# A hybrid attention layer on one Trainium2 core: matrix units moved between attention steps, x transposed two blocks at a time, one softmax sum folded into the norm

## Chip, cores and metric

The kernel runs on one core of one Trainium2 chip. The metric is the device time of one execution in microseconds (us), the median of several runs. All matrix products run on TensorE (PE in the profile); VectorE is DVE, ScalarE is ACT, GpSimd is POOL, and SP issues most of the loads.

## What is computed

One layer of a decoder for T = 512 positions and a width D of 1024, in float32. Cut to what matters:

```python
xn   = rmsnorm(h, g_attn)
proj = xn @ w_in                # q, k, v of 8 stick-breaking heads; q, k of 8 maps and v of 4 differential heads
sb   = stick_breaking(q, k, v)  # A[t,s] = beta_ts * prod over s<j<t of (1 - beta_tj), beta = sigmoid(z)
diff = (softmax(Q1 K1' / 8 + b1) - lam * softmax(Q2 K2' / 8 + b2)) V     # per head: two maps, 64 columns each
diff = rmsnorm(diff, g_subln) * (1 - lambda_init)
h    = h + concat(sb, diff) @ w_o
u    = causal_depthwise_conv3(rmsnorm(h, g_ffn) @ w_up)
h    = h + (gelu(gate) * val) @ w_down
h    = h + sigmoid(rmsnorm(h, g_ple) @ w_ple_gate) * (p @ w_ple_proj)
out  = rmsnorm(h, g_final)
```

`b1` and `b2` are biases by distance from a table of 32 rows; `lam` comes from four vectors of 64 numbers. All EPS are 1e-6.

## The kernel before

**Products.** A float32 product is made of three products of parts: each operand is split into a high part (`whi`, `xgh`, ...), a cast on ScalarE, and a low part (`wlo`, `xgl`, ...), a subtraction on VectorE. `mm3` (lines 119 to 123) issues the three matmuls. The attention's q, k and x come with 128 partitions by 512 positions in a tile.

**Weights as units.** `add_qk`, `add_v` and `add_wo` queue the projections as pieces. Their flow is a generator, and one `next` of it is a unit: one `mm3`, three matmuls of 512 columns. `units(n)` takes n of them from the flow; `rest()` takes what is left. Before a piece is used, its weights are loaded on SP's queue (`wraw`, line 131) and split (lines 140 and 141), two pieces ahead.

**Order.** TensorE's order is written by hand: it is the order of the code. The order on VectorE, ScalarE, GpSimd and SP is set by the scheduler of the framework, by priorities and by what a step needs. PSUM has two pools of tiles, `mm` (one bank, four tiles) and `z` (two banks, two tiles); which banks each gets is set by the one that is asked for first.

**Start** (`stages`, lines 715 to 772). x comes in four transfers. `warm(24)` runs 24 matmuls on an identity, `params_attn` transposes the gain `gattn`, and then `prep_x` (line 312) transposes a block of 128 columns of x into a PSUM bank and reads it twice, for `xgh` on ScalarE and `xgl` on VectorE. Two blocks share a tile `z`. `keep_x` reads it a third time and keeps a copy `xc` in DRAM for the residual. The first q and k products run between the later blocks. Then `units(8)`.

**Stick-breaking pairs** (`pair_steps`, line 535). A pair of heads goes through five steps: logits of two groups of rows with their sigmoids, scans and betas (`sb_sticks`, lines 510 to 518); the third group; transposes of the betas (line 562) in two steps; and `av` (line 574), whose eviction is two ScalarE copies (line 580) and two VectorE additions (line 581). A table `plan` of (pair, step, units) sets how many units follow each step.

**Parameters** (`params`, line 199) brings gains, convolution weights, the lambda vectors and the bias table; it transposes rows (lines 217 and 218), makes `sk` by two small matmuls (line 252) and copies it into `sk2` in DRAM (line 257), from which each head loads two strips on SP (line 595). It runs behind step 0 of pair 0.

**Differential heads** (`diff_steps`, line 587). Per row block and map: logits plus strip with a running minimum (line 618), exp with a row sum `sm` (line 622). The second map is scaled on ScalarE (line 627), and a VectorE operation scales the first and adds (line 628). Then transposes, `av`, the squares' sum by a matmul with ones (line 657), `rsqrt` (line 146), and the scaling by a broadcast row. A `plan` of (head, units) follows.

**Residual** (`residual`, line 668). An output tile is added to `hT` (line 671) on VectorE, then split into `h1` (lines 674 and 675). Behind the last of the eight tiles a new PSUM pool `psB` begins (line 826), and the up projection starts with its first two tiles.

Of the kernel before, what the change touches and what calls it, by code (L numbers as in the profile page):

```python
# [11 lines left out]
F32 = mybir.dt.float32  # L12
F32R = mybir.dt.float32r
AF = mybir.ActivationFunctionType
ALU = mybir.AluOpType
# [3 lines left out]
P = 128  # L19
T = 512  # L20
# [21 lines left out]
class Kern:  # L42
# [269 lines left out]
    def prep_x(self, pst):  # L312

        nc = self.nc
        self.xg_pool = self.open("xg", side="left")
        self.rst_pool = self.open("rst", side="left")
        self.xt_d = self.dram.tile([KT, P, T], F32, name="xt_d")
        self.xg = []
        for k in range(KT):
            ps = pst()  # L320
            for tb in range(NB):
                nc.tensor.transpose(ps[:, tb * P : (tb + 1) * P], self.xn[:, tb, k * P : (k + 1) * P], self.ident)
            hi = self.xg_pool.tile([P, T], F32R, name=f"xgh{k}")
            lo = self.xg_pool.tile([P, T], F32R, name=f"xgl{k}")
            g = self.gattn[:, k : k + 1]
            nc.scalar.activation(hi, ps, AF.Copy, scale=g)
            nc.vector.scalar_tensor_tensor(lo, ps, g, hi.bitcast(F32), op0=ALU.mult, op1=ALU.subtract)  # L327
            self.xg.append((hi, lo))
            yield ps

    def keep_x(self, k, ps):
        nc = self.nc
# [254 lines left out]
    def diff_steps(self, hd):  # L587
# [21 lines left out]
        for tb in (3, 2, 0, 1):  # L609
            if tb == 1:  # L610
                yield
                z.append(self.logits(q, k, groups[2]))
            n = (tb + 1) * P
            ts = [tiles[tb, j] for j in range(2)]
            bank, col = where[tb]
            for j in range(2):
                t = ts[j]
                nc.vector.tensor_tensor_reduce(
                    out=t, in0=z[bank][:, j, col : col + n], in1=strips[j][:, T - n : T], scale=-1.0, scalar=3e38,
                    op0=ALU.add, op1=ALU.min, accum_out=nm[:, j, tb : tb + 1],  # L620
                )
                nc.scalar.activation(t, t, AF.Exp, scale=-1.0, bias=nm[:, j, tb : tb + 1], accum_out=sm[:, j, tb : tb + 1])
            r = self.small.tile([P, 2], F32, tag="rsm", name=self.nm("rsm"))
            nc.vector.reciprocal(r, sm[:, :, tb])
            r1 = self.small.tile([P, 1], F32, tag="rlm", name=self.nm("rlm"))
            nc.vector.tensor_mul(r1, r[:, 1:2], self.neglam)
            nc.scalar.activation(ts[1], ts[1], AF.Copy, scale=r1)
            nc.vector.scalar_tensor_tensor(ts[0], ts[0], r[:, 0:1], ts[1], op0=ALU.mult, op1=ALU.add)
            pr[tb] = ts[0]
        yield  # L630

# [23 lines left out]
        ps = zo[:, 1, :] if hd == NDH - 1 else self.psm()  # L655
        for tb in range(NB):
            nc.tensor.matmul(ps[:, tb : tb + 1], lhsT=sq[:, tb * P : (tb + 1) * P], rhs=self.ones[:, 0:1], start=True, stop=True)
        rc = self.small.tile([P, NB], F32, tag="rcd", name=self.nm("rcd"))
        self.rsqrt(rc, ps[:, 0:NB], 1.0 / P)
        yield  # L660
        self.bcast_row(rc, ps)
        nc.vector.tensor_mul(o, ps, o)
# [32 lines left out]
    def stages(self):  # L695
# [18 lines left out]
        self.qks, self.v, self.hT, self.qk, self.late = {}, [None, None], None, None, []  # L714
        self.xn = self.su.tile([P, NB, D], F32, name="xn")
        self.load_x((0,))
        busy = self.psm()

        def warm(n):
            for _ in range(n):  # L720
                nc.tensor.matmul(busy[:, :P], lhsT=self.identR, rhs=self.identR, start=True, stop=True)

        warm(24)
        self.params_attn(psh)

        def first_load():
            cols = self.qk_cols(self.qoff[0], self.koff[0])
# [15 lines left out]
        self.add_wo(0, False, self.half_out)  # L743
        self.add_wo(4, True, lambda nt, ps: self.residual(nt, ps, "ffn", self.h1g, self.sqacc))
        self.load_raws(0)
        zs = [self.psz(), self.psz()]
        banks = [zs[0][:, 0, :], zs[0][:, 1, :], zs[1][:, 0, :], zs[1][:, 1, :]]
        banks = itertools.chain(banks, (f() for f in (self.psm, self.psm, psh, psh)))
        steps = self.prep_x(lambda: next(banks))
        self.prepare(2)  # L750
        first = [self.pieces[i][2](*self.splits[i]) for i in range(2)]
        todo = lambda i, n: [next(first[i], None) for _ in range(n)]
        px = [next(steps), next(steps)]
        warm(10)
        px += [next(steps), next(steps)]
        todo(0, 4)
        for k in range(2):
            self.keep_x(k, px[k])
        todo(1, 2)
        px += [next(steps), next(steps)]  # L760
        todo(1, 2)
        for k in range(2, 4):
            self.keep_x(k, px[k])
        px += [next(steps), next(steps)]
        self.norm_x()
        todo(0, 5)
        for k in range(4, KT):
# [22 lines left out]

        for evict in self.late:
            evict()
        self.units(8)
        pairs = [self.pair_steps(i) for i in range(4)]

        plan = [(0, 0, 4), (0, 1, 12), (0, 2, 4), (0, 3, 6), (1, 0, 4), (1, 1, 12), (0, 4, 6), (1, 2, 4), (1, 3, 6), (1, 4, 0)]
        for p in (2, 3):
            plan += [(p, 0, 4), (p, 1, 18), (p, 2, 4), (p, 3, 6), (p, 4, 0)]
        for i, (p, _, n) in enumerate(plan):
            next(pairs[p], None)  # L800
            self.units(n)
            if i == 0:
                self.params(self.psm)
        v = self.v[1] = self.vp.tile([P, NB, 2 * T], F32R, tag="v", name="v_diff")
        for i in range(2):
# [3 lines left out]


        heads = [self.diff_steps(i) for i in range(NDH)]
        plan = [(0, 2), (0, 12), (0, 5), (0, 2)]
        for h in range(NDH - 1):
            plan += [(h, 0), (h + 1, 2), (h + 1, 2), (h, 8), (h + 1, 5), (h + 1, 2)]
        plan += [(3, 6), (3, 0)]
        for h, n in plan:
            next(heads[h], None)
            self.units(n)
# [207 lines left out]
```

## Time and profile before

| what | value |
|---|---|
| runs | 726.16, 724.35 and 725.54 us, median 725.54 |
| the profiled execution | 726.1 us, of which the span of the trace is 724.3 us |
| mean granted TensorE clock | 0.988 |
| TensorE busy | 692.2 us (96%) |
| VectorE, ScalarE, GpSimd busy | 442.2 (61%), 319.2 (44%), 41.5 us (6%) |
| attention stage (from the first product to the last output tile) | 22 to 284 us |

The span runs from the first to the last instruction; what lies between it and the time of the execution is start and end of the program. Times in the rows below are on this trace's clock. A row with a bracket says how long the engine was idle ahead of it, and which instruction ended the wait; matmuls overlap, so that a product's own time is longer than the distance to the next one. PEclk 1.00 is 2.4 GHz and 0.50 is 1.2 GHz.

### The profile page before, as it was taken

The numbers are of one execution on the slowest core, as the hardware profiler recorded it, in microseconds if no ns is written. First come the engines' busy times: TensorE is split into PE (matmuls) and PEld (weight loads), VectorE is DVE, ScalarE is ACT, GpSimd is POOL, SyncE is SP. The second block draws the span as 40 slices with busy tenths as digits, with TensorE's granted clock in tenths as the row PEclk, the third lists the DMA queues.
The fourth block names the chain that finished last, engine by engine and source line by source line (L and its number), as shares of the span: only waits on it lengthen the run. The fifth ranks groups of instructions, "written<-read, shape, count | busy, mean of one in ns | idle before, by whom it ended". The sixth has DMA issues, their size and how long they took to land. (4 is left out here: it accounts for less than half of the span.)

```text
span 724.3 us, 8283 instructions
## 1 busy us (share of the span) xinstructions
PE 692.2 (96%) x3273; PEld 567.4 (78%) x3273; DVE 442.2 (61%) x667; ACT 319.2 (44%) x479; POOL 41.5 (6%) x52
## 2 busy tenths in 40 slices
PE   5899999999999997999999999999999999999995
PEld 4677787787887886888888888888888888888885
DVE  6267758376776649279767767767753342326435
ACT  3443545356666526155444444344432232326432
POOL 1300000000000005010000000000000010102001
PEclk9999999999999999899999999999999999999998
DMA  9244412222326111322233332233322331227102
GB/s 285 106 149 143 150 58 59 59 59 58 113 64 222 38 59 60 116 80 96 64 110 116 117 99 76 65 112 116 117 82 78 102 101 64 83 74 236 53 18 99
DMA packets 66809, 71.64 MB, mean 99 GB/s; under 512 B 2360, under 2 KB 55850, under 8 KB 66771
## 3 DMA queue, kind: packets, MB, share of 16 engines
q1 hardware_dynamic: 63376, 64.76, 28.0%
q10 hardware_dynamic: 2755, 4.27, 1.7%
q0 software_dynamic: 640, 2.10, 0.8%
q8 instruction: 25, 0.41, 0.2%
q14 instruction: 13, 0.11, 0.0%
HBM read 66.90 MB, written 6.84 MB: 102 GB/s over the span
## 5 line engine op out<-in xcount | busy, mean ns | idle before, releaser
L140 ACT CAST whi<-wraw 128x1024 fp32r<-128x1024 f32 (+1 forms) x102 | 105.5, 1034 | 166.9 <-PE mm L122 130.1
L141 DVE TENSOR_TENSOR wlo<-wraw,whi 128x1024 fp32r<-128x1024 f32 (+1 forms) x102 | 123.4, 1210 | 83.6 <-ACT whi L140 82.2
L121 PE MATMUL mm<-xgh,whi 128*128 128x512 f32 x128 | 54.2, 423 | 1.1 <-DVE v_sb L497 1.1
L123 PE MATMUL mm<-xgh,wlo 128*128 128x512 f32 x128 | 52.2, 408 | 0.0
L122 PE MATMUL mm<-xgl,whi 128*128 128x512 f32 x128 | 52.1, 407 | 0.0
L851 DVE TENSOR_TENSOR vpad<-mm,rb 128x512 f32<-128x512 f32 x44 | 30.1, 687 | 33.5 <-PE mm L123 33.3
L681 POOL TENSOR_TENSOR sqacc<-sqacc,sq 128x512 f32<-128x512 f32 x14 | 23.1, 1650 | 358.2 <-issue 254.9
L853 ACT ACTIVATE y<-vpad,par,par 128x512 f32<-128x512 f32 x44 | 35.5, 814 | 2.6 <-DVE vpad L851 2.5
L855 DVE SCALAR_TENSOR_TENSOR y<-vpad,par,y 128x512 f32<-128x512 f32 x44 | 33.0, 750 | 1.3
L854 DVE SCALAR_TENSOR_TENSOR y<-vpad,par,y 128x512 f32<-128x512 f32 x44 | 32.7, 745 | 0.0
L121 PEld LDWEIGHTS mm<-xgh,whi 128*128 128x128 f32 x128 | 25.4, 199 | 7.8 <-DVE v_sb L497 1.5
L123 PEld LDWEIGHTS mm<-xgh,wlo 128*128 128x128 f32 x128 | 25.2, 197 | 5.6
L857 ACT ACTIVATE y<-y 128x512 f32<-128x512 f32 x22 | 13.9, 632 | 35.1 <-DVE y L855 35.1
L122 PEld LDWEIGHTS mm<-xgl,whi 128*128 128x128 f32 x128 | 25.3, 198 | 4.9 <-DVE xgl L327 0.3
L517 DVE TENSOR_TENSOR_SCAN cum<-cum,fresh 128x512 f32<-128x512 f32 x20 | 23.6, 1212 | 5.9 <-ACT cum L510 5.9
L121 PE MATMUL mm<-whi,xgh 128*128 128x512 f32 x64 | 25.7, 401 | 1.6 <-DVE par L221 1.4
L532 DVE TENSOR_TENSOR twl<-z,twh 128x1024 fp32r<-128x1024 f32 (+2 forms) x20 | 18.4, 954 | 13.8 <-ACT twh L531 13.7
L478 PE MATMUL z<-k,q 64*128 64x512 f32 (+3 forms) x192 | 20.9, 342 | 4.8 <-DVE av L581 3.1
L123 PE MATMUL mm<-whi,xgl 128*128 128x512 f32 x64 | 25.0, 391 | 0.0
L122 PE MATMUL mm<-wlo,xgh 128*128 128x512 f32 x64 | 24.9, 390 | 0.0
L531 ACT CAST twh<-z 128x1024 fp32r<-128x1024 f32 (+2 forms) x20 | 15.2, 804 | 19.5 <-PE z L562 14.7
L478 PEld LDWEIGHTS z<-k,q 64*128 64x128 f32 x192 | 15.3, 189 | 10.4 <-issue 5.1
(535 smaller groups left out, 1778.0 us busy)
## 6 DMA issues: line engine op xcount, KB each, us to landing
wraw<-in_w_up SPq DMA_DIRECT2D x22, 1024.0 KB
wraw<-in_w_in SPq DMA_DIRECT2D x16, 512.0 KB
wraw<-in_w_down SPq DMA_DIRECT2D x8, 1024.0 KB
wraw<-in_w_in SPq DMA_DIRECT2D x4, 1024.0 KB
wraw<-in_w_o SPq DMA_DIRECT2D x4, 1024.0 KB
wraw<-in_w_ple_gate SPq DMA_DIRECT2D x4, 1024.0 KB
wraw<-in_w_down SPq DMA_DIRECT2D x4, 768.0 KB
sk<-sk ACTq DMA_DIRECT2D x1, 2560.0 KB
```

What stands on the lines that cost most here:

```text
L121: nc.tensor.matmul(ps, lhsT=l[0], rhs=r[0], start=start, stop=False, **kw)
L122: nc.tensor.matmul(ps, lhsT=l[0], rhs=r[1], start=False, stop=False, **kw)
L123: nc.tensor.matmul(ps, lhsT=l[1], rhs=r[0], start=False, stop=stop, **kw)
L140: nc.scalar.copy(hi, raw)
L141: nc.vector.tensor_sub(lo, raw, hi.bitcast(F32))
L478: nc.tensor.matmul(z[:, h, col : col + n], lhsT=q[o, x, tb * P : (tb + 1) * P], rhs=k[o, y, :n], start=i == 0 and at == 0, stop=i == 2 and ...
L517: nc.vector.tensor_tensor_scan(back, back, fresh, 1.0, op0=ALU.mult, op1=ALU.max)
L681: nc.gpsimd.tensor_add(sqacc, sqacc, sq)
L851: nc.vector.tensor_mul(u[:, 2 : T + 2], ps, rb2)
L853: nc.scalar.activation(y, u[:, 2 : T + 2], AF.Identity, scale=self.cw(2, ch), bias=self.g("cb", ch))
L854: nc.vector.scalar_tensor_tensor(y, u[:, 1 : T + 1], self.cw(1, ch), y, op0=ALU.mult, op1=ALU.add)
L855: nc.vector.scalar_tensor_tensor(y, u[:, 0:T], self.cw(0, ch), y, op0=ALU.mult, op1=ALU.add)
```

## The change

`prep_x` transposes two blocks into two banks, both before either is read. The double tiles `z` are asked for ahead of the `mm` tiles, the warming matmuls go from 24 + 10 to 12 + 8 + 4, and four blocks of x stand ahead of the first product. The numbers of units in both plans change, 8 become 7 ahead of the pairs, and `params` runs at entry 8 of the plan. In a head, the first map stays unscaled: the second one is scaled by (sum of the first) x (-lam) / (sum of the second) while it is added, and the first sum, squared, multiplies EPS in the norm.

```diff
-        for k in range(KT):
-            ps = pst()
-            for tb in range(NB):
-                nc.tensor.transpose(ps[:, tb * P : (tb + 1) * P], self.xn[:, tb, k * P : (k + 1) * P], self.ident)
...
+        for k0 in range(0, KT, 2):
+            banks = [pst(), pst()]
+            for i, ps in enumerate(banks):
+                for tb in range(NB):
+                    k = k0 + i
+                    nc.tensor.transpose(ps[:, tb * P : (tb + 1) * P], self.xn[:, tb, k * P : (k + 1) * P], self.ident)
+            for i, ps in enumerate(banks):
...
+            yield banks
...
-            r = self.small.tile([P, 2], F32, tag="rsm", name=self.nm("rsm"))
-            nc.vector.reciprocal(r, sm[:, :, tb])
+            r = self.small.tile([P, 1], F32, tag="rsm", name=self.nm("rsm"))
+            nc.vector.reciprocal(r, sm[:, 1, tb : tb + 1])
             r1 = self.small.tile([P, 1], F32, tag="rlm", name=self.nm("rlm"))
-            nc.vector.tensor_mul(r1, r[:, 1:2], self.neglam)
-            nc.scalar.activation(ts[1], ts[1], AF.Copy, scale=r1)
-            nc.vector.scalar_tensor_tensor(ts[0], ts[0], r[:, 0:1], ts[1], op0=ALU.mult, op1=ALU.add)
+            nc.vector.scalar_tensor_tensor(r1, sm[:, 0, tb : tb + 1], self.neglam, r, op0=ALU.mult, op1=ALU.mult)
+            nc.vector.scalar_tensor_tensor(ts[0], ts[1], r1, ts[0], op0=ALU.mult, op1=ALU.add)
...
-        self.rsqrt(rc, ps[:, 0:NB], 1.0 / P)
+        e = self.small.tile([P, NB], F32, tag="rce", name=self.nm("rce"))
+        nc.vector.scalar_tensor_tensor(e, sm[:, 0, :], EPS, sm[:, 0, :], op0=ALU.mult, op1=ALU.mult)
+        nc.vector.scalar_tensor_tensor(e, ps[:, 0:NB], 1.0 / P, e, op0=ALU.mult, op1=ALU.add)
+        nc.gpsimd.tensor_tensor(rc, e, self.mhalf[:, :NB], op=ALU.pow)
...
+        zs = [self.psz(), self.psz()]
         busy = self.psm()
...
-        warm(24)
-        self.params_attn(psh)
+        warm(12)
+        self.params_attn(lambda: zs[1][:, 0, :])
...
-        zs = [self.psz(), self.psz()]
...
-        px = [next(steps), next(steps)]
-        warm(10)
-        px += [next(steps), next(steps)]
+        px = next(steps)
+        warm(8)
+        px += next(steps)
+        warm(4)
         todo(0, 4)
...
-        self.units(8)
+        self.units(7)
...
-        plan = [(0, 0, 4), (0, 1, 12), (0, 2, 4), (0, 3, 6), (1, 0, 4), (1, 1, 12), (0, 4, 6), (1, 2, 4), (1, 3, 6), (1, 4, 0)]
+        plan = [(0, 0, 3), (0, 1, 12), (0, 2, 4), (0, 3, 4), (1, 0, 3), (1, 1, 18), (0, 4, 4), (1, 2, 4), (1, 3, 4), (1, 4, 4)]
         for p in (2, 3):
-            plan += [(p, 0, 4), (p, 1, 18), (p, 2, 4), (p, 3, 6), (p, 4, 0)]
+            plan += [(p, 0, 3), (p, 1, 13), (p, 2, 4), (p, 3, 4), (p, 4, 4 if p == 2 else 9)]
...
-            if i == 0:
+            if i == 8:
                 self.params(self.psm)
...
-        plan = [(0, 2), (0, 12), (0, 5), (0, 2)]
+        plan = [(0, 3), (0, 11), (0, 5), (0, 2)]
...
-        plan += [(3, 6), (3, 0)]
+        plan += [(3, 7), (3, 0)]
```

What this does to the order of instructions shows at three places. First, TensorE at the start. Before (`xn` is x, `xgh` and `xgl` are its parts, `whi` and `wlo` those of the first q weights):

```order
L721 MATMUL mm_101<-identR 128x128 x24
L196 MATMUL z_129<-ident,rows_126 128x8
L322 MATMUL z_138<-ident,xn 128x128 x8
L721 MATMUL mm_101<-identR 128x128 x10
L322 MATMUL z_139<-ident,xn 128x128 x8
L121 MATMUL mm_206<-xgh_168,whi_140 128x512
L122 MATMUL mm_206<-xgl_169,whi_140 128x512
```

and with the change:

```order
L730 MATMUL mm_103<-identR 128x128 x12
L196 MATMUL z_102<-ident,rows_116 128x8
L324 MATMUL z_101<-ident,xn 128x128 x8
L730 MATMUL mm_103<-identR 128x128 x8
L324 MATMUL z_102<-ident,xn 128x128 x8
L730 MATMUL mm_103<-identR 128x128 x4
L121 MATMUL mm_195<-xgh_159,whi_127 128x512
L122 MATMUL mm_195<-xgl_160,whi_127 128x512
```

The count of transposes ahead of the first product is the same, 16; between the two blocks of a tile there is no longer a read to wait for, and the warming matmuls stand at three places.

Second, ScalarE in the first pair: `cum` and `beta` are the sigmoids of a group's logits `z`, `lexp` is the Exp for lambda. Before:

```order
L374 CAST q_419<-qkt_420 128x512
L238 ACTIVATE lexp<-lsum 128x2
L510 ACT_TABLE_LOAD
L510 ACTIVATE cum_366<-z_424 128x1024
L511 ACTIVATE beta_448<-z_424 128x1024
L510 ACTIVATE cum_367<-z_433 128x1024
L511 ACTIVATE beta_454<-z_433 128x1024
```

and with the change:

```order
L514 ACT_TABLE_LOAD
L514 ACTIVATE cum_356<-z_406 128x1024
L515 ACTIVATE beta_430<-z_406 128x1024
L238 ACT_TABLE_LOAD
L238 ACTIVATE lexp<-lsum 128x2
L514 ACT_TABLE_LOAD
L514 ACTIVATE cum_357<-z_415 128x1024
L515 ACTIVATE beta_436<-z_415 128x1024
```

The Exp moved in between the two groups, and with it two table loads.

Third, TensorE at the end of the attention stage: the last output tile (with `mix`), and the first two tiles of the up projection (with `h1`), with the semaphores that they wait for. Before:

```order
L123 MATMUL mm_2507<-mix7h_2378,wlo_2352 128x512
L121 MATMUL mm_2595<-h10h,whi_2591 128x512 [waits DVE_49,Activation_49]
L122 MATMUL mm_2595<-h10l,whi_2591 128x512
...
L121 MATMUL mm_2595<-h13h,whi_2591 128x512 [waits Activation_49]
L122 MATMUL mm_2595<-h13l,whi_2591 128x512
L123 MATMUL mm_2595<-h13h,wlo_2592 128x512
L121 MATMUL mm_2612<-h10h,whi_2608 128x512 [waits Activation_49]
```

and with the change:

```order
L123 MATMUL mm_2485<-mix7h_2353,wlo_2330 128x512
L121 MATMUL mm_2573<-h10h,whi_2569 128x512 [waits Activation_49]
L122 MATMUL mm_2573<-h10l,whi_2569 128x512 [waits DVE_49]
...
L121 MATMUL mm_2573<-h13h,whi_2569 128x512 [waits Activation_49]
L122 MATMUL mm_2573<-h13l,whi_2569 128x512 [waits DVE_49]
L123 MATMUL mm_2573<-h13h,wlo_2570 128x512
L121 MATMUL mm_2590<-h10h,whi_2586 128x512 [waits DVE_49,Activation_49]
```

The wait for VectorE's last addition to `hT` stands at the first product of the first tile before, and at that of the second tile with the change. The waits of the first tile for VectorE are now for `h1` and `wlo`.

On the other queues, the strips of head 0 move on SP from ahead of the loads of the second half of v's weights to behind them, ahead of the next q and k weights, and the copy into `sk2` moves on ScalarE's queue to between the two `av` copies of pair 1.

## Rows read from the trace of the kernel before

**Rows 1.** Page, part 1: busy time, share of the span and instructions of each engine.
```profile
PE 692.2 (96%) x3273; PEld 567.4 (78%) x3273; DVE 442.2 (61%) x667; ACT 319.2 (44%) x479; POOL 41.5 (6%) x52
```

**Rows 2.** Waits of TensorE: total us, times, longest us.
```profile
PE z L322 <- DVE xgl L327: 6.6, 2, 5.1
...
PE z L478 <- DVE av L581: 3.1, 2, 1.6
PE z L639 <- DVE pr L628: 2.2, 2, 1.7
PE z L322 <- ACT xc L334: 2.2, 1, 2.2
...
PE z L478 <- DVE nmx L618: 1.7, 1, 1.7
PE mm L121 <- DVE par L221: 1.4, 1, 1.4
PE mm L121 <- DVE v_sb L497: 1.1, 1, 1.1
```

**Rows 3.** Timeline of TensorE, start and pair 0: start us, us, operation, count.
```profile
1.91 5.38 PE L721 MATMUL mm<-identR 128*128 128x128 f32 x24 [1.91 <-DVE identR L181]
...
7.42 1.11 PE L322 MATMUL z<-ident,xn 128*128 128x128 f32 x4
...
21.62 1.11 PE L322 MATMUL z<-ident,xn 128*128 128x128 f32 x4 [1.57 <-DVE xgl L327]
22.38 0.78 PE L121 MATMUL mm<-xgh,whi 128*128 128x512 f32 x1
...
27.65 0.41 PE L121 MATMUL mm<-xgh,whi 128*128 128x512 f32 x1
...
29.06 1.04 PE L322 MATMUL mm<-ident,xn 128*128 128x128 f32 x8
...
64.96 1.91 PE L562 MATMUL z<-ident,beta 128*128 128x128 f32 x16
```

**Rows 4.** Timeline of ScalarE at the start, the third set's cast.
```profile
14.81 1.05 ACT L140 CAST whi<-wraw 128x1024 fp32r<-128x1024 f32 x1 [3.21 <-DMA wraw<-in_w_in]
```

**Rows 5.** Timeline of VectorE at the start, the same set's subtraction.
```profile
15.89 1.22 DVE L141 TENSOR_TENSOR wlo<-wraw,whi 128x1024 fp32r<-128x1024 f32 x1 [0.28 <-ACT whi L140]
```

**Rows 6.** Windows: us, PE, PEld, DVE, ACT, POOL busy, PEclk, DMA.
```profile
109.60:113.00 3.40, 1.84 (x18) 1.62 (x18) 2.40 (x4) 3.09 (x5) 0.00 (x0) 1.00 0.02 5
113.00:116.40 3.40, 3.40 (x10) 2.62 (x9) 3.30 (x4) 2.12 (x3) 0.00 (x0) 0.50 0.00 0
177.90:181.30 3.40, 3.40 (x13) 2.24 (x12) 2.87 (x9) 3.39 (x8) 0.00 (x0) 0.50 0.00 0
287.00:290.50 3.50, 2.59 (x6) 2.16 (x7) 2.61 (x4) 3.30 (x5) 1.28 (x1) 0.51 0.02 5
290.50:293.90 3.40, 3.40 (x9) 2.66 (x9) 2.13 (x2) 0.02 (x1) 1.41 (x1) 0.50 0.51 156
```

**Rows 7.** Timeline of ScalarE in pair 0, the table load.
```profile
48.28 1.28 ACT L510 ACT_TABLE_LOAD   x1
49.58 1.02 ACT L510 ACTIVATE cum<-z 128x1024 f32<-128x1024 f32 x1
```

**Rows 8.** Timeline of TensorE and VectorE ahead of the up projection.
```profile
287.91 0.77 PE L121 MATMUL mm<-h10h,whi 128*128 128x512 f32 x1 [3.98 <-DVE hT L671]
...
286.49 1.27 DVE L671 TENSOR_TENSOR hT<-mm,hT 128x512 f32<-128x512 f32 x2
```

**Rows 9.** Timeline of VectorE, pair 0's last beta.
```profile
61.74 0.69 DVE L518 TENSOR_TENSOR beta<-beta,cum 128x512 f32<-128x512 f32 x1
```

**Rows 10.** Groups of instructions: count, busy us, mean ns, idle time ahead.
```profile
L627 ACT ACTIVATE pr<-pr,rlm 128x512 f32<-128x512 f32 (+3 forms) x16 | 8.7, 555 | 3.5 <-DVE rlm L626 3.1 <-DVE rsm L624 0.3
```

**Rows 11.** Timeline of the queues: the bias copy, and its first reader.
```profile
60.41 0.75 ACTq L257 DMA_DIRECT2D sk<-sk  x1
...
77.44 0.82 SPq L595 DMA_DIRECT2D strip<-sk  x2
```

More of the change, by code (lines that the diff above doesn't have):

```diff
@@ L318, in prep_x @@
         self.xg = []
-        for k in range(KT):
-            ps = pst()
-            for tb in range(NB):
-                nc.tensor.transpose(ps[:, tb * P : (tb + 1) * P], self.xn[:, tb, k * P : (k + 1) * P], self.ident)
[L323 to L329, printed above, removed]
+        for k0 in range(0, KT, 2):
[5 more added lines that the diff above has]
+            for i, ps in enumerate(banks):
+                k = k0 + i
+                hi = self.xg_pool.tile([P, T], F32R, name=f"xgh{k}")
+                lo = self.xg_pool.tile([P, T], F32R, name=f"xgl{k}")
+                g = self.gattn[:, k : k + 1]
+                nc.scalar.activation(hi, ps, AF.Copy, scale=g)
+                nc.vector.scalar_tensor_tensor(lo, ps, g, hi.bitcast(F32), op0=ALU.mult, op1=ALU.subtract)
+                self.xg.append((hi, lo))
+            yield banks
     def keep_x(self, k, ps):
@@ L759, in stages @@
         todo(1, 2)
-        px += [next(steps), next(steps)]
+        px += next(steps)
         todo(1, 2)
@@ L763, in stages @@
             self.keep_x(k, px[k])
-        px += [next(steps), next(steps)]
+        px += next(steps)
         self.norm_x()
```

## Prediction

> **What bounds the kernel now.** I read the busy line of the page first: TensorE works 692.2 us of a span of 724.3, the next engine, VectorE, 442.2 [rows 1]. So time is won only where TensorE stands still or runs slowly. Some 30 us of standing still are left. The waits view of TensorE [rows 2] names most of them; the start of the program leads (5.1 and 1.5 for xgl, 2.2 for xc), then come seven waits of 0.5 to 1.7 us in the attention stage, and one of 3.98 ahead of the up projection, which the timeline shows [rows 8]. Second, the rows of the start show a slow TensorE: from 22.38 to 27.65 twelve products take 5.27 us, 0.44 each; then six take 1.41, 0.235 each [rows 3]. This is half clock and full clock (1.2 and 2.4 GHz). The windows show three falls to 0.50 later: at 113.0, at 177.9 and from 287.1 to 293.9 [rows 6]. Each follows one of the waits: the first for av (1.6), that for nmx (1.7) and the one of 3.98. The 1.4 for par, the second for av, as long as the first, and the 1.7 for pr brought none [rows 2]. Work done at 0.50 takes twice as long, so 3.4 us of it lose 1.7.
>
> The sum is made against the profiled execution: 726.1 us of its own, 0.56 above the median of the three runs, 725.54. Below, "now" is a time on the clock of the trace of before. No change under 0.3% (2.2 us) can be told from none.
>
> **The start.** Before, blocks 0 and 1 of x are transposed, then TensorE waits 5.1 us for the first two reads of them, and again for each later pair. The change puts blocks 0 to 3, which now have both double banks, ahead of the first product, with 24 warming matmuls instead of 34. TensorE comes to that product after 1.91 + 24 x 0.224 + 16 x 0.277 = 11.7 us [rows 3], not at 22.38. It then runs into its operands: the third set of weights lands late, and its cast runs from 14.81 to 15.86 [rows 4]; behind it come one xgh (0.69), the wlo (1.22 from 15.9) and two xgl (0.7 each, as other reads of 512 columns [rows 9]) on VectorE [rows 5], 18.6 in all. With the last products at half clock the twelfth ends near 19.5, not 27.65: 8.2 us earlier. This is not the gain, for it depends on when the clock rises. Before, it rose 6.0 us after the last idle gap of the start (21.62 to 27.65), and at the third fall 6.0 us after work resumed (287.91 to 293.9) [rows 3, 8]. Counted from 18.6 to 19.5 the rise comes near 25, when 8 more products and 8 more transposes are done than before had at its own rise, and before had done these by 27.65 + 8 x 0.235 + 0.8 = 30.3: 5.3 us won. I take 4.3, with 1 us off for a wait on the transposes of blocks 4 and 5. Each us by which the clock rises later costs half a us: with a rise at 22 it is 5.3 + 1.5 = 6.8, with one only in the long run of q and k products, near 33, 5.3 - 4.0 = 1.3. These are the ends.
>
> **Pair 0.** The parameters' transposes and their wait (1.4) [rows 2] leave this place. But two table loads come in on ScalarE: the Exp for lambda now stands between the two groups' sigmoids. One load took 1.28, and the next instruction began 0.02 behind it [rows 7]. The second group's sigmoid thus comes between 50 and 51.4 (51.4 before) though the first starts earlier; the scans on VectorE follow it, and the pair's last beta, ready at 62.4 before [rows 9], ends between 58 and 60.5. TensorE reached its transposes at 64.96 [rows 3]; without 5 units (15 products, 3.5), the parameters' own 1.2 and the wait it is there at 58.8. It waits 1.7 at the late end, which I take because three loads now share ScalarE with this chain, and nothing at the early end. Against the 1.4 of before that is +0.3. Ends: 1.4 won, 1.3 lost. The Trainium skill ("ScalarE: Activation LUTs", section "What ACT_TABLE_LOAD costs") puts a drain of about 1.38 us on top of each load, which speaks against this change; by it the pair would lose another 2.8, and the sum be 13.5 instead of 16.3. The trace leaves no room for it.
>
> **Pairs 1 to 3 and head 0.** The v_sb wait of 1.1 goes, as VectorE has 9 units' time for it ahead of the av: -1.1. Between the av of one pair and the logits of the next, where nothing stood, are now 4 units, 12 products, 2.8 us at 0.235. The first wait for av lies wholly behind them: -1.6. Ahead of pair 3 a weight's wlo now stands between the two av additions on VectorE, so of 1.5 about 0.6 stays: -0.9. At head 0 the wait of 1.7 (for nmx, in truth for the v_diff and av behind it) goes with 9 units ahead of head 0, but these logits need the k of this head, whose last product ends 2 us ahead and whose eviction on VectorE stands behind the av additions, two v_diff and a wlo. By rows of the same sizes [rows 5, 9] VectorE has five operations of 0.7 and three of 1.2, 7.1, and 1.0 of ScalarE's copies between them, 8.1 us; TensorE's 27 products take 6.3: a wait of 1.8, +0.1. Each of these two can go from 1 us won to 3 lost.
>
> **Clock of this stage.** The fall behind the first wait for av goes (-1.7). Of waits near 1.6 about half brought one, so the new wait of head 0 keeps its fall at even odds (-0.85), and that of pair 0 brings one at even odds (+0.85): -1.7. The Trainium skill ("TensorE: Matmul & The Clock Gate", section "Why this matters for your kernels") asks only that idle gaps stay below a length that is longer than 1.6 and 1.7 us. By it these falls have another cause and stay: the sum would be 14.6. The trace has a fall right behind each of the two waits [rows 2, 6], though also equal waits without one, so I stay with the rows.
>
> **Heads.** The sixteen ScalarE copies of the second map (8.7 us) [rows 10] go; they lay between exp and the combination that the transposes wait for (2.2 us in two waits) [rows 2]. In their place each head gets one more VectorE operation on four columns. Both waits should go, but head 3 gains about 0.8 from hT additions that VectorE does first, and a little stays: -1.2, between 0 and -2.2. Of the norm only the operations change: tensor_scalar is exchanged for two small ones, beside 8 units. Moving the parameters costs nothing at its new place: a unit or more covers each eviction, and the bias copy lands about 122, with its first use behind 175. That cover gone, the cost would be the 1.4 of pair 0 again.
>
> **Ahead of the up projection.** TensorE stops at 283.93 for the last residual's addition, which ends at 287.76 [rows 8], since the first up tile gets the PSUM bank of the last output tile. The order with its waits shows this wait moved to the second tile, for the two pools have changed banks. The twelve products of the first tile (2.8 us) come before it: 1.1 us is left with the start of the pipe, -2.9. A wait of 1.1 is shorter than any that brought a fall, so the 6.0 us of work at half clock behind it take 3.0: -3.0. If VectorE is late by 1 us more the first is -1.9.
>
> **Sum.** -4.3 + 0.3 - 1.1 - 1.6 - 0.9 + 0.1 - 1.7 - 1.2 - 2.9 - 3.0 = -16.3; 726.1 - 16.3 = **709.8 us**.
>
> **Rivals.**
> *The clock stays low through the start.* The transposes and warming matmuls don't raise it; it rises when the q and k products run without a stop. For: after 24 warming matmuls, 5.38 us without a gap, four transposes took 1.11 us, while eight at full clock took 1.04 [rows 3]. Against: the products of before did raise it. The start gives 1.3, the time is 712.8. The Trainium skill says of transposes that they do not engage the full clock as products do ("TensorE: Matmul & The Clock Gate", section "Part 4: PE-mode transpose"); the rows agree as far as they go. Chance 0.26.
> *The waits come back on VectorE.* Units that no longer stand ahead of the transposes leave the scans and the softmax uncovered: TensorE waits there for what it no longer waits for at the logits. Pairs 1 to 3 and the heads give nothing, -4.7 and the clock's -1.7 are lost, and pair 0 loses up to 1 more: 716.2 to 717.2. For: VectorE worked 2.40 of 3.40 us around 110 and 3.30 of the next 3.40 [rows 6]. Against: over the span it works 61% [rows 1]. Chance 0.13.
> *Nothing changes.* TensorE only arrives earlier at a chain of VectorE that sets the end of the attention stage: the last additions run back to back with no idle time ahead [rows 8]. What is won upstream is then waited for ahead of the second up tile, the clock falls there as before, and the time is 725. Against: that chain is fed by TensorE's own output tiles. Chance 0.04.
> *Slower: a late bias copy.* The strips of head 0 stand on SP's queue until the copy is there, issued at 60.41 and waited for until 77.44, 17 us [rows 11]. Now the copy goes out near 105, between the two av copies of pair 1, and the strips stand ahead of weights that TensorE wants about 133. At 17 us these arrive some 5 us early. It decides from 22 us on; each us more is one of TensorE's, and beside the weights' transfers 41 us would give 709.8 + 19 = 728.8. Chance 0.03.
>
> **The numbers.** Forecast 0.54, the others 0.26, 0.13, 0.04, 0.03. The forecast's own range is 705 to 713: the start at 7 and neither wait nor fall in pair 0 give 709.8 - 2.5 - 1.7 - 0.9 = 704.7, both falls and 1.5 us more of waiting 709.8 + 1.7 + 1.5 = 713. 705 to 720 takes in the first two rivals as well, with some 0.1 left out. Faster: 0.54 + 0.26 + 0.13 less a trifle, 0.92; same 0.05; slower 0.03.
>
> **What would show it.** Right: the first product near 12 us and the twelfth by 20; full clock by 25 (rival one: not before 32); no wait for xgl above 3 us; no wait at the logits of pair 2; a wait of about 2 us ahead of the transposes of pair 0, behind three table loads; 0.50 gone at 113 and from 287 on; the first up tile running at once, with about 1 us ahead of the second. Wrong: a fall of the clock ahead of the up projection still there, new waits for VectorE in the heads of more than 4 us in all, or SP waiting for the bias copy while TensorE waits for weights.

## The result, and the profile after

The changed kernel takes 706.44 us (median of four runs, 705.81 to 707.91) against 725.56 before: a ratio of 0.9741, 95% interval 0.9721 to 0.9762. A second set of runs of it, taken with the last experiments, gave 706.84 and 0.975 (0.9725 to 0.9774). Forecast were 709.8 and a range of 705 to 720, so the forecast lies 3.4 us too high. The span of the trace went from 724.3 to 704.3.

Page of the changed kernel, part 1; it answers to [rows 1]:

```profile
PE 684.6 (97%) x3263; PEld 561.2 (80%) x3263; DVE 443.1 (63%) x671; ACT 315.3 (45%) x465; POOL 42.5 (6%) x52
```

TensorE is busy for 7.6 us less, since its products run at full clock for longer and ten warming matmuls are gone (x3263 against x3273), and idle for the other 12.4 us less. The waits view of TensorE, which answers to [rows 2] (`beta` is what the transposes of a pair read, `k` a head's keys after their split, `nmx` the running minimum of a head's logits, `pr` a head's map after exp, `par` the transposed parameters, `v_sb` the v of the pairs, `qkt` a q or k before its split):

```profile
PE z L566 <- DVE beta L522: 2.3, 1, 2.3
PE mm L122 <- DVE xgl L331: 2.0, 3, 0.9
PE mm L730 <- DVE identR L181: 1.9, 1, 1.9
PE z L482 <- DVE k L379: 1.7, 1, 1.7
PE mm L121 <- ACT xgh L330: 1.5, 1, 1.5
PE mm L121 <- DVE hT L679: 1.3, 1, 1.3
PE z L482 <- DVE av L585: 0.6, 1, 0.6
PE z L482 <- DVE nmx L622: 0.5, 1, 0.5
```

The 5.1 us for xgl, the first wait for av, and those for par, v_sb and pr are gone. What is left in the attention stage are the beta of pair 0, the k of head 0, a rest of the av of pair 2, and 0.5 for nmx in head 1. The timeline of TensorE at the start answers to [rows 3]:

```profile
4.87 1.97 PE L324 MATMUL z<-ident,xn 128*128 128x128 f32 x8
...
10.22 1.10 PE L730 MATMUL mm<-identR 128*128 128x128 f32 x4
11.12 0.73 PE L121 MATMUL mm<-xgh,whi 128*128 128x512 f32 x1
...
12.51 0.56 PE L121 MATMUL mm<-xgh,whi 128*128 128x512 f32 x1
13.94 0.50 PE L122 MATMUL mm<-xgl,whi 128*128 128x512 f32 x1 [0.88 <-DVE xgl L331]
...
16.82 0.79 PE L121 MATMUL mm<-xgh,whi 128*128 128x512 f32 x1 [1.46 <-ACT xgh L330]
18.48 0.79 PE L122 MATMUL mm<-xgl,whi 128*128 128x512 f32 x1 [0.87 <-DVE xgl L331]
...
19.50 0.63 PE L121 MATMUL mm<-xgh,whi 128*128 128x512 f32 x1
```

The first product stands at 11.12, the twelfth is through at 19.5. And the windows of the changed kernel, cut at the changes of the clock and behind the waits (columns as in [rows 6]):

```profile
12.90:16.20 3.30, 1.58 (x6) 0.82 (x5) 3.23 (x9) 2.15 (x4) 1.28 (x2) 1.00 1.19 307
16.40:23.00 6.60, 5.32 (x14) 3.93 (x15) 4.00 (x12) 1.54 (x3) 2.15 (x3) 0.50 0.68 259
23.20:30.00 6.80, 6.51 (x33) 4.70 (x32) 2.91 (x4) 4.85 (x9) 1.29 (x3) 1.00 0.21 80
54.30:57.70 3.40, 3.39 (x23) 3.10 (x24) 2.84 (x4) 1.96 (x3) 0.00 (x0) 1.00 0.28 66
163.50:166.90 3.40, 3.40 (x25) 3.02 (x26) 2.42 (x11) 1.69 (x5) 0.00 (x0) 1.00 0.00 0
273.50:277.00 3.50, 3.50 (x16) 2.87 (x16) 2.76 (x3) 2.60 (x4) 2.06 (x2) 1.00 0.02 5
```

The clock is at 1.00 from 12.9, falls at 16.3, within the second of two waits (0.9 and 1.5 us), and is at 1.00 again from 23.1 to 698.9, where before it rose at 27.65. (Ahead of its first rise the column prints 1.00 too; there the products tell: up to 12.51 they stand 0.43 apart, which is half clock.) In this execution no wait behind that brings a fall: not the 2.3 us of pair 0 (ends at 54.3), not the 1.7 of head 0 (163.5), not the 1.3 ahead of the second up tile (273.5).

**Where the 20.0 us of span went.** The first product of the up projection moved from 287.91 [rows 8] to 269.30, 18.6 us earlier. 4.0 of it is the wait ahead of it. 5.6 is the start: the broadcast of the norm, which has the same 42 products and 32 transposes ahead of it in both, begins at 30.88 instead of 36.51. The waits between these two places fell from 9.7 to 5.1 us, and two falls of the clock, 1.7 each, went. These make 17.6; about 1 us stays without a name. Behind that point the wait for the second tile costs 1.3, and 3.0 are won from the fall that is gone: 436.4 us from there to the end before, 435.0 now.

### The profile page after: what moved, and what is told of

It reads as the page before. It is cut to its first block, busy times and chain, and to the rows that moved or that the text cites. A ratio compares the mean times of both kernels' runs of the same rounds, so it can differ in the third digit from the quotient of the medians.

```text
span 704.3 us, 8234 instructions
## 1 busy us (share of the span) xinstructions
PE 684.6 (97%) x3263; PEld 561.2 (80%) x3263; DVE 443.1 (63%) x671; ACT 315.3 (45%) x465; POOL 42.5 (6%) x52
## 5 line engine op out<-in xcount | busy, mean ns | idle before, releaser
L689 POOL TENSOR_TENSOR sqacc<-sqacc,sq 128x512 f32<-128x512 f32 x14 | 23.1, 1652 | 359.0 <-issue 254.9
L626 ACT ACTIVATE pr<-pr,nmx 128x512 f32<-128x512 f32 (+3 forms) x32 | 17.7, 555 | 12.6 <-DVE nmx L622 12.4
L536 DVE TENSOR_TENSOR twl<-z,twh 128x1024 fp32r<-128x1024 f32 (+2 forms) x20 | 18.5, 953 | 5.2 <-ACT twh L535 5.0
```

The costliest lines, as they stand in the source:

```text
L689: nc.gpsimd.tensor_add(sqacc, sqacc, sq)
```

## The experiments

Each has one part of the change undone, done alone or replaced, or something added to the changed kernel. Ratios are to the kernel before, run on the same chip; the changed kernel stands at 0.9741 and 0.975. Differences in us are between medians; the medians of the kernel before lie between 725.18 and 726.44 in these sets, so about 1 us of such a difference can be the chip's. Where a kernel's difference to the changed one is under about 0.3%, the trace decides.

**The order of the PSUM pools alone**, in the kernel before (the transposes of the gain `gattn` into zs[1] go with it):

```diff
+        zs = [self.psz(), self.psz()]
         busy = self.psm()
...
-        self.params_attn(psh)
+        self.params_attn(lambda: zs[1][:, 0, :])
...
-        zs = [self.psz(), self.psz()]
```

> The kernel before, with only the order of the two PSUM pools changed (the double tiles are asked for first). Theory: the wait ahead of the up projection falls from 3.98 us to about 1.3, since twelve products of the first tile no longer stand behind the last residual's addition, and the stretch at 0.50 behind it (6.0 us of work) goes too: 725.6 - 2.7 - 3.0 = 719.9. Rival one, the clock falls there whatever the length of the wait: 722.9. Rival two, the addition itself sets the end and the wait only moves to the second tile: 725.5.

Measured: 722.37 us, 0.996 (0.9947 to 0.9973). The waits of TensorE in the profile:

```profile
PE z L322 <- DVE xgl L327: 9.4, 3, 5.1
PE z L639 <- DVE pr L628: 3.3, 3, 1.7
...
PE mm L122 <- DVE h17l L675: 1.1, 1, 1.1
```

The wait for hT is not in the list at all: here even the second tile got a bank whose reader is an earlier addition, and what TensorE waits for is the low part of the last one, 1.1 us. The clock is at 1.00 from 181.9 to the last stretch. From the place where TensorE comes to the up projection (283.9 before, 285.7 here) to the end of the span it is 440.4 us before and 434.9 here: 5.5, as the theory has it (5.7). But TensorE comes there 1.8 us later, with 1.1 more for pr in head 0 and 0.5 for qkt in pair 0, for the scheduler set some instructions of VectorE in another order; the start lost nothing (the broadcast is 0.4 earlier). So the mechanism holds at its size, and a third of it was lost upstream. The time lies at that of rival one, but by the trace no fall is left there.

**The pools in the old order**, in the changed kernel:

```diff
-        zs = [self.psz(), self.psz()]
         busy = self.psm()
+        zs = [self.psz(), self.psz()]
```

> The changed kernel with the old order of the pools. Theory: the wait ahead of the up projection is 4.0 us again instead of 1.3, with a fall of the clock behind it: 706.4 + 2.7 + 3.0 = 712.1. Rival, only the wait returns: 709.1.

Measured: 710.7 us, 0.98 (0.9786 to 0.9815), 4.3 us over the changed kernel. The wait is back, and so is a fall; its windows around head 0 and ahead of the up projection:

```profile
163.00:164.50 1.50, 1.50 (x18) 1.45 (x18) 0.53 (x1) 0.00 (x0) 0.00 (x0) 1.00 0.00 0
164.60:168.00 3.40, 3.40 (x12) 2.63 (x10) 3.17 (x16) 3.30 (x11) 0.00 (x0) 0.50 0.00 0
273.86:277.20 3.34, 3.34 (x8) 2.67 (x9) 2.44 (x3) 3.21 (x5) 1.28 (x1) 0.50 0.02 5
```

The wait is 3.4 us, since TensorE arrives 1.0 later than in the changed kernel, and the fall behind it lasts 3.4 us. From its arrival to the end of the span it is 438.5 us here and 434.8 in the changed kernel: 3.7 us are the pools' own, and the rest lies upstream. The middle row holds something else: behind head 0's wait of 1.71 us, the same to a hundredth as in the changed kernel, the clock fell here and did not there.

**The old numbers of units**, in the changed kernel:

```diff
-        self.units(7)
+        self.units(8)
...
-        plan = [(0, 0, 3), (0, 1, 12), (0, 2, 4), (0, 3, 4), (1, 0, 3), (1, 1, 18), (0, 4, 4), (1, 2, 4), (1, 3, 4), (1, 4, 4)]
+        plan = [(0, 0, 4), (0, 1, 12), (0, 2, 4), (0, 3, 6), (1, 0, 4), (1, 1, 12), (0, 4, 6), (1, 2, 4), (1, 3, 6), (1, 4, 0)]
...
-            plan += [(p, 0, 3), (p, 1, 13), (p, 2, 4), (p, 3, 4), (p, 4, 4 if p == 2 else 9)]
+            plan += [(p, 0, 4), (p, 1, 18), (p, 2, 4), (p, 3, 6), (p, 4, 0)]
...
-        plan = [(0, 3), (0, 11), (0, 5), (0, 2)]
+        plan = [(0, 2), (0, 12), (0, 5), (0, 2)]
...
-        plan += [(3, 7), (3, 0)]
+        plan += [(3, 6), (3, 0)]
```

> The changed kernel with the old numbers of units (8 ahead of the pairs, the old plans; the parameters stay at entry 8). Theory: waits for av return at pair 2 and pair 3 (1.5 each, together 2.4 more than now), v_sb costs 1.1 again, and pair 0's wait of 2.3 shrinks by the two units more that stand ahead of it, 1.4: 706.4 + 2.1 = 708.5 if the clock stays up, as it did behind waits of 1.7 and 2.3 in the changed kernel. Rival, a wait of 1.5 brings a fall by its length: two falls more, 1.7 each, 712.

Measured: 713.08 us, 0.9836 (0.9822 to 0.9851), 6.6 over the changed kernel. Its waits of TensorE:

```profile
PE z L482 <- DVE av L585: 3.1, 2, 1.6
...
PE z L482 <- ACT beta L515: 2.4, 1, 2.4
PE z L482 <- DVE nmx L622: 2.1, 2, 1.7
...
PE mm L121 <- DVE v_sb L501: 0.2, 1, 0.2
```

Both waits for av and the one for nmx are back as in [rows 2]. In pair 0 the wait moved to the third group's logits, which need the `z` tile that ScalarE's last beta still reads. The time is that of the rival with two falls, but not by its rule: the clock fell around the 2.4 us (0.50 from 45.4 to 52.2) and behind the 1.7 (171.7 to 175.1), which together cost 5.0 us, and not behind either wait of 1.55. The waits themselves are 9.0 us from pair 0 on, against 6.4 in the changed kernel, and the start came 1.0 earlier. So of the 6.6 us only 2.6 are waits; most of it is falls that the changed kernel's profiles don't have, though these have waits of 2.3 and 1.7 us too.

**The old end of the softmax**, in the changed kernel:

```diff
-            r = self.small.tile([P, 1], F32, tag="rsm", name=self.nm("rsm"))
...
-            nc.vector.scalar_tensor_tensor(ts[0], ts[1], r1, ts[0], op0=ALU.mult, op1=ALU.add)
+            r = self.small.tile([P, 2], F32, tag="rsm", name=self.nm("rsm"))
...
+            nc.scalar.activation(ts[1], ts[1], AF.Copy, scale=r1)
+            nc.vector.scalar_tensor_tensor(ts[0], ts[0], r[:, 0:1], ts[1], op0=ALU.mult, op1=ALU.add)
...
-        nc.gpsimd.tensor_tensor(rc, e, self.mhalf[:, :NB], op=ALU.pow)
+        self.rsqrt(rc, ps[:, 0:NB], 1.0 / P)
```

> The changed kernel with the old softmax end (sixteen ScalarE copies, both maps scaled, tensor_scalar in the norm). Theory: the waits for pr at the transposes of the heads return in part, 1.3 us: 707.7. Rival, the units alone took those waits away: 706.4, with no wait for pr in the trace.

Measured: 708.49 us, 0.9781 (0.9757 to 0.9805). One row of its waits settles it:

```profile
PE z L644 <- DVE pr L633: 1.7, 2, 0.9
```

The changed kernel has no such row. The fold takes away 1.7 us of waiting, of the 2.0 measured; the 8.7 us of ScalarE work [rows 10] as such were worth nothing.

**The parameters at entry 0**, in the changed kernel:

```diff
-            if i == 8:
+            if i == 0:
```

> The changed kernel with the parameters at entry 0 of the plan again. Theory: in pair 0 the parameters' work (some 1.9 us of TensorE and 3 units) comes back ahead of its transposes, so the wait of 2.3 us for the last beta there goes, and the wait of 1.4 for par comes in its place: 706.4 less 0 to 1, so 705.9. Rival, VectorE holds the pair back whatever stands ahead: both waits in full, 707.8.

Measured: 705.56 us, 0.9713 (0.9698 to 0.9729). The wait for the last beta of pair 0 is gone from its list, 0.7 us in two waits and 0.8 for an av came, and TensorE reaches pair 2's logits at 102.22, in the changed kernel at 102.36. So moving the parameters gave nothing: at entry 0 their own TensorE work covers what pair 0 waits for otherwise. By the ratio this kernel is even 0.3% below the changed one, at the edge of what can be told.

**The old start**, in the changed kernel, with the pools in the new order:

```diff
-        for k0 in range(0, KT, 2):
-            banks = [pst(), pst()]
+        for k in range(KT):
+            ps = pst()
...
-        warm(12)
+        warm(24)
...
-        px = next(steps)
-        warm(8)
-        px += next(steps)
-        warm(4)
+        px = [next(steps), next(steps)]
+        warm(10)
+        px += [next(steps), next(steps)]
```

> The changed kernel with the old start (24 + 10 warming matmuls, transposes in single blocks), the pools in the new order. Theory: the products begin at 22 again and the broadcast of the norm, reached at 30.9 now, at 36.5: 706.4 + 5.6 = 712.0. Rival, what the start wins is waited for in pair 0 (2.3 us of wait go): 709.7.

Measured: 711.47 us, 0.9803 (0.9777 to 0.9829), 4.6 to 5.0 over the changed kernel. TensorE waits 10.4 us for xgl in three waits, and the 2.1 us of pair 0 stay. The gain of the start arrives at the end; the rival falls. (The profiled execution is the slowest of the four, 714.61: its broadcast comes at 37.88, and the clock falls behind the 2.1 us of pair 0.)

**Six warming matmuls in the gap**, in the changed kernel:

```diff
-        todo(0, 4)
+        todo(0, 3)
+        warm(6)
+        todo(0, 1)
```

> The changed kernel with six more warming matmuls behind the ninth product, in the wait of 1.46 us ahead of the tenth, after which the clock fell. Theory: TensorE's idle time there brings the fall, and without it the work from 16.8 to 23.1 runs at full clock: up to 2 us less, 704.9. Rival, the fall stands for the waits of this whole stretch or for none of them: no change, 706.4.

Measured: 705.92 us, 0.9717 (0.9703 to 0.9732), not clear of the changed kernel by time. TensorE at the gap, and a window in pair 0:

```profile
16.30 0.63 PE L123 MATMUL mm<-xgh,wlo 128*128 128x512 f32 x1
16.73 1.38 PE L730 MATMUL mm<-identR 128*128 128x128 f32 x6
17.90 0.73 PE L121 MATMUL mm<-xgh,whi 128*128 128x512 f32 x1
...
19.30 0.39 PE L123 MATMUL mm<-xgh,wlo 128*128 128x512 f32 x1
```

```profile
52.80:56.00 3.20, 3.18 (x15) 3.20 (x16) 1.77 (x3) 1.01 (x1) 0.00 (x0) 0.50 0.23 55
```

The broadcast came at 29.23 instead of 30.88: 1.65 us won at its place, the size that was expected, but not in the way that was expected. In this execution the clock was not up ahead of the gap (the products stand 0.43 apart up to 16.3); it rose once, at 18.5, and stayed up to pair 0, so there was no fall here for the matmuls to prevent. Then the clock fell behind pair 0's wait of 2.3 us, where it did not in the changed kernel, and that cost the profiled execution 1.6 us. It does not explain the time alone: two of the four executions had a mean clock of 0.998 against its 0.995, and took 705.27 and 705.69.

**The Exp on GpSimd**, in the changed kernel, so that the table loads of pair 0 go:

```diff
-        nc.scalar.activation(e, s, AF.Exp)
+        base = c.tile([P, 2], F32, name="ebase")
+        nc.gpsimd.memset(base, math.e)
+        nc.gpsimd.tensor_tensor(e, base, s, op=ALU.pow)
```

> The changed kernel with the Exp for lambda made by GpSimd's power, so that the two more table loads of pair 0 go. Theory as predicted: the loads hold the second group's sigmoids and with them the beta that TensorE waits 2.3 us for: 704.3. Rival, read from the trace of the changed kernel: VectorE's queue was busy without a break and took the scan at once, so the loads cost nothing: 706.4.

Measured: 702.49 us, 0.9667 (0.9649 to 0.9685), less than either theory had, and not for either reason. The second sigmoid came 2.6 us earlier, at 42.97 instead of 45.59, and the wait in pair 0 did not shrink but went from 2.3 to 3.2 us. The timeline of ScalarE in the changed kernel:

```profile
40.83 1.03 ACT L514 ACTIVATE cum<-z 128x1024 f32<-128x1024 f32 x1
...
42.78 1.28 ACT L238 ACT_TABLE_LOAD   x1
44.08 0.20 ACT L238 ACTIVATE lexp<-lsum 128x2 f32<-128x2 f32 x1
44.30 1.28 ACT L514 ACT_TABLE_LOAD   x1
45.59 1.03 ACT L514 ACTIVATE cum<-z 128x1024 f32<-128x1024 f32 x1
```

and that of VectorE, which shows why:

```profile
42.42 0.23 DVE L233 CUSTOM_DVE_ANT_0 mix4l<-mix4l 128x64 f32<-128x64 f32 x1 [1.92 <-DMA mix4l<-in_lambda_k]
...
42.57 2.34 DVE L521 TENSOR_TENSOR_SCAN cum<-cum,fresh 128x512 f32<-128x512 f32 x2
...
46.66 2.34 DVE L521 TENSOR_TENSOR_SCAN cum<-cum,fresh 128x512 f32<-128x512 f32 x2
```

VectorE stands still for the lambda vectors until 42.42, though the first group's sigmoid ended at 41.86: that costs the first scan 0.7 us. From there it has no idle time to 54.1. It takes the second group's scan at 46.66, when the sigmoid ends at 46.62: the loads were covered, if barely. With GpSimd's power, VectorE waited 0.9 us longer for it, and the last beta came 1.3 us later though the sigmoid came 2.6 earlier. The two loads took 1.28 us each and the next instruction began 0.02 and 0.01 us behind; of the drain that the Trainium skill gives for it ("ScalarE: Activation LUTs", section "What ACT_TABLE_LOAD costs") these rows show nothing.

The 4 us came from elsewhere. By operand, products of the changed kernel against this one are equal but for three kinds, mix, act and h2. The new tile of two columns (`base`) had moved the weights by 32 bytes.

**That tile alone**, in the changed kernel:

```diff
         self.ident = c.tile([P, P], F32, name="ident")
+        self.pad = c.tile([P, 2], F32, name="pad")
+        nc.gpsimd.memset(self.pad, 0.0)
```

> The changed kernel with one tile of two columns more among the constants, which nothing reads. It moves all tiles behind it by 32 bytes, weights and gains' products among them, and changes nothing else. Theory from the run with the Exp on GpSimd, in which a product with mix, act or h2 as an operand took 227 ns from start to start instead of 234, and where the weights lay as those operands do by their address modulo 64: 893 products of 7 ns less and what stands beside them, 4 to 5 us less than the changed kernel, 702. Rival, that gain came with the Exp: 706.4.

Measured: 702.85 us, 0.9681 (0.9659 to 0.9704); the changed kernel beside it 706.84. Groups of products in the changed kernel (count, busy us, mean ns):

```profile
L122 PE MATMUL mm<-h14l,whi 128*128 128x512 f32 x44 | 17.1, 389 | 0.0
...
L123 PE MATMUL mm<-gwh,h23l 128*128 128x512 f32 (+1 forms) x9 | 3.3, 371 | 0.0
...
L121 PE MATMUL mm<-act0h,whi 128*128 128x512 f32 x8 | 3.2, 396 | 0.0
```

and the same groups with the pad:

```profile
L122 PE MATMUL mm<-h14l,whi 128*128 128x512 f32 x44 | 17.1, 389 | 0.0
...
L123 PE MATMUL mm<-gwh,h23l 128*128 128x512 f32 (+1 forms) x9 | 3.3, 365 | 0.0
...
L121 PE MATMUL mm<-act0h,whi 128*128 128x512 f32 x8 | 3.1, 389 | 0.0
```

By the addresses in the built programs, the weights `whi` and `wlo` of the changed kernel start on a multiple of 64 bytes in a partition (37056), and act and mix 32 bytes past one (139232, 200672); x and h1 lie as these weights do. The third kind, h2, lies on a multiple too, but its weights (`gwh`) are 32 past. With the pad, `whi`, `wlo`, x, h1 and h2 move to 32 past, and all of them agree. Products of 128x512 whose two operands agree take 389 ns, whether both are on 0 or both on 32; those whose operands differ took 394 to 396, 7 ns more from start to start too (234 against 227). Distances other than 32 bytes were not tried. The trace has 888 such products: 6.2 us. From the first product of the up projection to the end, where the clock is equal in both, it is 434.9 us in the changed kernel run beside it and 430.8 with the pad; upstream of it, what the mix products give is taken back by a fall of the clock in pair 0 (0.50 from 53.9 to 57.3). The kernel before pays the same (230 to 238 from start to start), so this has no part in what the change gave.

The profile with the pad shows one thing more, at the start:

```profile
9.74 0.64 PE L732 MATMUL mm<-identR 128*128 128x128 f32 x4
10.21 0.45 PE L121 MATMUL mm<-xgh,whi 128*128 128x512 f32 x1
```

The last four warming matmuls took 0.64 us, where in the changed kernel they took 1.10: here the clock was up before the first product.

**More units shifted**, in the changed kernel:

```diff
-        plan = [(0, 0, 3), (0, 1, 12), (0, 2, 4), (0, 3, 4), (1, 0, 3), (1, 1, 18), (0, 4, 4), (1, 2, 4), (1, 3, 4), (1, 4, 4)]
+        plan = [(0, 0, 3), (0, 1, 15), (0, 2, 4), (0, 3, 4), (1, 0, 3), (1, 1, 15), (0, 4, 4), (1, 2, 4), (1, 3, 4), (1, 4, 4)]
...
-            plan += [(p, 0, 3), (p, 1, 13), (p, 2, 4), (p, 3, 4), (p, 4, 4 if p == 2 else 9)]
+            plan += [(p, 0, 3), (p, 1, 13 if p == 2 else 11), (p, 2, 4), (p, 3, 4), (p, 4, 6 if p == 2 else 12)]
...
-        plan = [(0, 3), (0, 11), (0, 5), (0, 2)]
+        plan = [(0, 0), (0, 11), (0, 5), (0, 2)]
```

> The changed kernel with three units moved from pair 1 to ahead of pair 0's transposes, and units moved to ahead of the logits of pair 3 and head 0 (6 for 4, 12 for 9). Theory: the waits of 2.3, 0.65 and 1.7 us shrink by the 3, 2 and 3 units' 2.1, 1.4 and 2.1 us: 4.2 less, 702.2. Rival, fewer units behind them lay VectorE bare: the waits come back at v_sb, at pair 3's transposes or in head 0, 706.

Measured: 703.51 us, 0.969 (0.9669 to 0.971). Waits for k and av are gone, 0.6 for nmx came in head 0, and in pair 0 1.6 us for qkt stand where 2.3 for beta stood: TensorE now arrives at a bank that VectorE, in the same unbroken row of work, has not emptied. It gave 3.3 us of the expected 4.2.

**All that gave something, together**: pad, shifted units, warming matmuls in the gap, and

```diff
-            products(sp, ps, range(KT // 2 if n < 2 else KT))
+            products(sp, ps, range((5, 4)[n] if n < 2 else KT))
...
-                for _, _, ps, sp in held:
-                    products(sp, ps, range(KT // 2, KT))
+                for j, (_, _, ps, sp) in enumerate(held):
+                    products(sp, ps, range((5, 4)[j], KT))
```

> The changed kernel with the pad, the shifted units, six warming matmuls in the gap of the start, and five instead of four sets of products of the first up tile ahead of the second. Theory, the parts add up: 4.5 + 4.2 + 1.7 + 0.7 = 11.1 less, 695.3. Rival, waits return between them: 698 to 700.

Measured: 697.82 us, 0.962 (0.9601 to 0.9639), 9.0 less than the changed kernel beside it. Its waits:

```profile
PE mm L122 <- DVE xgl L333: 2.7, 3, 1.3
...
PE mm L121 <- DVE qkt L379: 1.6, 1, 1.6
PE z L484 <- DVE nmx L624: 1.1, 2, 0.6
PE mm L121 <- DVE hT L681: 0.9, 1, 0.9
PE mm L121 <- ACT xgh L332: 0.9, 1, 0.9
```

Of the sum of the parts, 11.1 us, 9.0 came, a trifle more than the rival had; singly the pad gave 4.0, the units 3.3, and the warming matmuls 1.65 at their place. The wait for hT is 0.9 against 1.6 with the pad alone, so the fifth set of products took off the 0.7 that was expected. The warming matmuls left waits of 0.9 and 1.1 us in the gap, and the clock, which was up ahead of them here, fell again (0.50 from 19.0 to 22.4).

**The changed kernel once more**, on the same chip as the last three:

> The changed kernel as it is, beside the three others on one chip, for their differences. Theory: 706.4, with the same waits; a fall of the clock may stand behind another of them, as waits of 1.7 and 2.3 us had one in some kernels and none in others.

Measured: 706.84 us, from pair 0 on with the waits of its first profile to a tenth, but for 0.5 more at the third group's logits in pair 0. At the start the clock rose once, at 23.7, and not for a while at 12.9, and it did not fall again before 699.6; the broadcast came at 31.11, 0.2 later than in the first profile.

## Why the prediction was right, and where it was off

- **Start** (-4.3 said, -5.6 measured). First product and twelfth came as worked out (11.7 and 19.5 said). The step that was mis-sized is the rise of the clock, put 6.0 us behind the last wait, at 25: it was 23.1, 4.6 us behind that wait, which makes 1 us of the difference; in the eight other profiles of this start with nothing put into the gap it came 3.1 to 5.9 us behind it. Of the 1 us taken off for a wait behind the later transposes, 0.3 came. The 3.4 us at full clock from 12.9 on gave next to nothing: without them, in the second profile of the same kernel, the broadcast came 0.2 later. The rival of a clock that stays low until 32 falls. Its premise falls too: in the changed kernel the clock was up when only three products and part of a fourth had followed 24 warming matmuls and 16 transposes, and with the pad it was up ahead of the first product, after warming matmuls and transposes alone. Which of the two raised it the runs don't separate, so the sentence of the Trainium skill that transposes do not count as products do ("TensorE: Matmul & The Clock Gate", section "Part 4: PE-mode transpose") is neither borne out nor refuted here.
- **Pair 0** (+0.3 said, +0.8 measured). The size was near by luck, for the cause was wrong: "three loads now share ScalarE with this chain" fell with the Exp on GpSimd. VectorE's queue held the pair back, first behind the transfer of the lambda vectors (0.7 us), then by its own work, without a break from 42.4 on.
- **Pairs 1 to 3 and head 0.** v_sb and the first av gone, 0.6 left of the second and 1.7 for k in head 0: all as forecast to 0.1.
- **Clock of the attention stage** (-1.7 said, -3.4 in the profile). The step that failed is that a fall goes with the length of the wait, at even odds near 1.6. A wait of 1.71 us at head 0 had a fall behind it in the experiments on the old pools and the old units, and none in the changed kernel; 2.3 us in pair 0 had one in the profile with the warming matmuls, and none in either profile of the changed kernel. Counted over all fourteen profiles, behind the start: the clock fell at 6 of 25 waits of 1.5 to 1.8 us, at 4 of 8 of 2.1 to 2.5, at all three of 3.2 to 4.0, and at none of the shorter ones. The executions of one kernel differ too: the four of the pad had mean clocks of 0.987 to 0.989 and 702.53 to 703.94 us, but for one with 0.997 and 700.21. So this term is no property of the kernel to within 3 us, and what decides it the runs don't show. The rule of the Trainium skill weighed against it ("TensorE: Matmul & The Clock Gate", section "Why this matters for your kernels") would have said 0 here, and falls behind 1.56 and 1.71 us speak against that too.
- **Heads** (-1.2 said, -1.75 measured). Both waits for pr went; the 0.8 put on head 3 did not come, 0.5 for nmx did in head 1. The undone softmax shows that the fold took these 1.7 us away.
- **Ahead of the up projection** (-2.9 and -3.0 said, -2.7 and -3.0 measured). As forecast, with the pool order alone as its cause.
- **Other rivals.** The bias copy took 15 us at its new place and no weights were late. Behind head 0's, the heads got one new wait for VectorE, of 0.5 us. The parts undone one at a time cost 4.3 (pools), 6.6 (units), 2.0 (softmax) and 4.6 to 5.0 (start), and nothing for the parameters: 17.5 to 18 of the 19.1. That they nearly add up is in part luck, since 1.7 of the pools' 4.3 and 5.0 of the units' 6.6 are, in their profiles, falls of the clock upstream of the up projection.

Against the profiled execution (706.0) the forecast was 3.8 us too high: 1.3 are the start's, 1.7 the clock's, 0.5 the heads', and about 1 has no name; pair 0 and the second tile took back 0.7.

## What to carry to other kernels

Read a moved instruction on every queue that it joins: the lambda vectors and their two small reductions stood in the first pair's VectorE work, where they cost 0.7 us, while the ScalarE loads that caught the eye cost nothing. The order in which two PSUM pools are first asked for sets whose eviction the next stage's first tile waits for; in the traces that was worth 3.7 to 5.5 us here. A term that hangs on the clock falling or not behind a wait of 1.5 to 2.5 us should carry both values in the range, not a mean.

## What the runs showed that was not expected

Products of 128x512 in these three-part sums took 389 ns when the stationary and the moving operand start alike past a multiple of 64 bytes in their partitions, and 394 to 396 when one starts 32 bytes further: 4.0 us of the kernel's time, from one unread tile of two columns. And behind waits of equal length the clock fell in some profiles and not in others, and one kernel's executions differed in their mean clock by 0.01 and in their time by 3 us.
